# A decoder layer on one core: the second products of a tile group in a bank of their own, later table turning, and other rates for the weight sums

## The chip, the cores and the metric

The kernel runs on one core of a Trainium2 chip, as one launch. The metric is the device time of a run in microseconds. The kernel before took 1041.94 us (median of three runs: 1041.69, 1041.94, 1045.71). Everything said of single instructions comes from one further execution that the hardware profiler recorded.

## The reference

One layer of a decoder is computed for 512 positions of width 1024, in 32-bit floats. A combined projection gives queries, keys and values for three causal mixers and three gate vectors; the branches are projected, gated, summed and projected again; after a layer norm come a squared-ReLU MLP of width 4096, a gated embedding and a second layer norm. Cut to its frame:

```python
proj = x @ w_in
(da_q, da_k, da_v, sb_q, sb_k, sb_v, dl_q, dl_k, dl_v, gates) = jnp.split(proj, _split_points(), axis=-1)
...
o_da = diff_attention(da_q, da_k, da_v, lam, da_norm, rel_bias[:, :DA_HEADS], lam_init)
o_sb = stick_breaking_attention(sb_q, sb_k, sb_v)
o_dl = dilated_attention(dl_q, dl_k, dl_v, rel_bias[:, DA_HEADS:])
g = jax.nn.sigmoid(gates)
merged = g[0] * (o_da @ w_branch_da) + g[1] * (o_sb @ w_branch_sb) + g[2] * (o_dl @ w_branch_dil)
x = layer_norm(alpha * x + merged @ w_out, ln1_g, ln1_b)
c = jnp.square(relu(x @ w_up)) @ w_down
x = layer_norm(alpha * x + c + sigmoid(x @ w_ple_gate) * (p @ w_ple), ln2_g, ln2_b)
```

The differential attention (`da`) has four heads with two softmax maps each, the dilated one (`dl`) three groups of four heads. Both add a relative bias that depends on the distance alone; the kernel makes a table of it by loading shifted rows (tiles `sh`, from the DRAM vector `rv`) and reversing them on VectorE (tiles `shf`).

## The kernel before, in words

**Products.** Each 32-bit operand is split in a high and a low part, and each product is made of three matmuls: `mm3` (L87) issues them at L88, L89 and L90. Weights come in chunks of 128 x 1024 (512 KB): SyncE loads a chunk into `raw` (L214, six buffers), ScalarE (ACT) casts the high part `wh` (L262), VectorE (DVE) subtracts for the low part `wl` (L264). `wh` and `wl` have five buffers each, so the cast of a chunk waits for the last product with the chunk five before it.

**Seven instead of eight.** Most projections use a form with seven products on quarters of the operands instead of eight. It needs sums of weight quarters; these are made in DRAM by DMAs with addition that GpSimd (POOL) issues, in 200 steps: L1284 for a plain copy, L1282 for an addition. The tiles are `vsum`, `qsum`, `msum`, `bsum`, `gsum`, and for the MLP `usum` and `dsum`.

**The main stream.** The work is a list of items, each with its products (`mm`) and its evacuation (`ev`), which is recorded after the products of the next item have got their chunks. Per item n a credit grows by its size times its rate, and for each whole credit one sum step is issued; a manual dependency ties each step to a low part made shortly before. Attention heads are generators that are advanced a step at a time beside the items (`step()`); a generator in `pending` is advanced once a step too. The order on each engine is what comes of this recording and of a scheduler behind it, and is fixed before the run.

**Items.** The first are plain tiles, then three groups of eight items (`group_items`, at items 53, 61 and 69): a pair of dilated query and key tiles, differential heads 0 and 1, differential heads 2 and 3. Then come gates and branches: `gate_alone` (77 to 104), a first branch (105 to 112), `branch_seven` (113 to 126), `gate_chain` (127 to 140), `branch_seven` (141 to 158), the output projection, and the MLP from about item 180 to 317.

**One group.** For j = 0, 1 (two pairs of query and key tiles) the seven products, called by their numbers 1 to 7, are made with 128 x 256 results. Their order is: product 2 (`of_two`), 1 (`of_one`), 7 and 6 (`of_seven_six`), 5 (`of_five`), 3 and 4 (`of_three_four`). PSUM has two banks for results of this kind (`mm`) and six for all else (`at`, among them the attention logits). Product 2 goes into the left half (`HB`) of an `mm` bank, ACT copies it to `gs` (L419), and product 1 then goes into the same half of the same bank. DVE adds the two (`put`, L390, into `da_q` or `dl_q`); product 7, on the operand `u7h`, continues in this bank and so waits for the put. After the group, `doubled` makes the forms that the differential logits want: `da_qa`, `da_qb` from `da_q` (L102, L109, L110), then high and low parts of `da_k` (L401, L405 on ACT; L102 and L406 on DVE, tile `da_kl`). The logits are L147 and L148.

**Tables.** `da_tables` issues four loads of 256 KB on POOL (L1719) for the differential heads, at item `DA_TABS` = 58; `turn_da` records their four reversing copies on DVE (L1729), at item 62. The tables of the dilated heads were loaded the same way much earlier (items 9 to 22). L2052 adds a dilated table to logits, in softmax steps of a dilated head.

Of the kernel before, what the change touches and what calls it, by code (L numbers as in the profile page):

```python
# [13 lines left out]
AF = mybir.ActivationFunctionType  # L14
# [42 lines left out]
def trunk(tc, a, out):  # L57
    nc = tc.nc
    es = ExitStack()
    with es:  # L60
# [14 lines left out]
        def slot(name, dt=F32):  # L75
            return big.tile([P, 512], dt, name=nm(name), tag="s", bufs=NSLOT)
# [4 lines left out]
        def mm_bank():  # L81
            return psum.tile([P, 512], F32, name=nm("mm"), tag="mm", bufs=2)

        def at_bank():
            return psum.tile([P, 512], F32, name=nm("at"), tag="at", bufs=6)

        def mm3(ps, wh, wl, xh, xl, start, stop):  # L87
            nc.tensor.matmul(ps, wh, xh, start=start, stop=False, skip_group_check=True)  # L88
            nc.tensor.matmul(ps, wh, xl, start=False, stop=False, skip_group_check=True)  # L89
            nc.tensor.matmul(ps, wl, xh, start=False, stop=stop, skip_group_check=True)  # L90
# [193 lines left out]
        items = []  # L284
# [24 lines left out]
        scale = {"da_q": 0.125, "sb_q": 0.125, "dl_q": 128.0 ** -0.5}  # L309
# [39 lines left out]
        HB = slice(0, 256)  # L349
# [3 lines left out]
        def group_items(gi, pairs):  # L353
# [11 lines left out]
                    return ps.rearrange("p (n c) -> p c n", c=4)  # L365
                return ps

            def prod(j, p, c, start, stop):
                ch = cs[p][0]
                for k in range(4):  # L370
                    s = slice(512 * j + k * P, 512 * j + k * P + P)
                    mm3(both[j]["x"][:, c], ch["h"][:, s], ch["l"][:, s], *xf[p][k], start and k == 0, stop and k == 3)

            def add(ps, need, free, run, ev, bank):
                for p in ps:
                    at = {5: 0, 6: 1, 7: 2, 3: 3}.get(p)
                    cs[p] = [chunk(w[{1: 0, 2: 1, 4: 3}[p]] if at is None else qsum[gi][at], 1024)]
                item([c for p in free for c in cs[p]], lambda b: run(), lambda b: ev(),
                     need=[c for p in need for c in cs[p]], bank=bank)
                items[-1]["rate"] = 0.6  # L380
# [13 lines left out]
            def doubled(j):  # L394

                T[pairs[j][0]] = evac_stacked(out[j][0], "da_q", scale["da_q"])
                yield
                t = out[j][1]
                hi, lo = [[slot(n, F32R) for _ in range(2)] for n in ("da_k", "da_kl")]
                for i, c in enumerate((A, B)):  # L400
                    nc.scalar.activation(hi[i][c], t[c], AF.Copy, scale=-1.0)  # L401
                    sub_hi(lo[i][c], t[c], -1.0, hi[i][c])
                yield
                for i, (c, d) in enumerate(((A, B), (B, A))):
                    nc.scalar.copy(hi[i][d], hi[i][c].bitcast(F32))  # L405
                    nc.vector.tensor_copy(lo[i][d], lo[i][c].bitcast(F32))  # L406
                T[pairs[j][1]] = list(zip(hi, lo))
                yield

            def of_two():  # L410
                def run():
                    for j in range(2):
                        b = both[j]
                        if j:
                            b["x"] = mm_bank()
                        prod(j, 2, HB, True, True)
                        b["s"] = slot("gs")
                        sc = -scale[pairs[j][0][0]] if pairs[j][0][0] == "dl_q" else 1.0
                        nc.scalar.activation(b["s"][:, HB], b["x"][:, HB], AF.Copy, scale=sc)  # L419

                def ev():
                    for j in range(2):
                        for i in range(2):
                            out[j][i] = slot(pairs[j][i][0])

                def bank():
                    both[0]["x"] = mm_bank()
                    return both[0]["x"]
                add((2,), (2,), (2,), run, ev, bank)

            def of_one():
                def run():
                    for j in range(2):
                        prod(j, 1, HB, True, False)
                        if not j:
                            put(0, 0, 0, both[0]["x"][:, HB], both[0]["s"][:, HB])

                def ev():
                    put(1, 0, 0, both[1]["x"][:, HB], both[1]["s"][:, HB])
                add((1,), (1,), (1,), run, ev, lambda: both[0]["x"])  # L440

            def of_seven_six(j):
                def run():
# [327 lines left out]
        def seven(forms, operand, bank_of, done):  # L771

            cs = {}
            for p in (1, 2, 7, 6, 4, 5, 3):
                for r in range(2):
                    if not r:
                        cs[p] = [operand(cs, p, kp) for kp in range(2)]

                    def mm(ps, p=p, r=r):
                        q = slice(r * P, r * P + P)  # L780
                        for k in range(4):
                            c = cs[p][k // 2]
                            n = slice(k % 2 * 512, k % 2 * 512 + 512)
                            h, lo = forms[p][k]
                            go, end = k == 0 and p in bank_of["first"], k == 3 and p in bank_of["last"]
                            nc.tensor.matmul(ps, h[:, q], c["h"][:, n], start=go, stop=False, skip_group_check=True)
                            nc.tensor.matmul(ps, h[:, q], c["l"][:, n], start=False, stop=False, skip_group_check=True)  # L787
                            nc.tensor.matmul(ps, lo[:, q], c["h"][:, n], start=False, stop=end, skip_group_check=True)

                    def bank(p=p, r=r):  # L790
                        return bank_of["get"](p, r)

                    def ev(ps, p=p, r=r):
                        done(ps, p, r)
                    if p == 5:
                        bank_of.get("sums", set()).add(len(items))
                    item(cs[p] if r else [], mm, ev, need=cs[p], bank=bank, size=0.5)
                    items[-1]["rate"] = 1.0

        msum = [[[dram.tile([P, 1024], F32, name=f"msum{n}_{m}_{i}") for i in range(2)] for m in range(2)]  # L800
                for n in range(3)]
# [128 lines left out]
        def branch_seven(i, behind):  # L930

            s, b, cs = {}, {}, {}
            for p in (2, 1, 7, 6, 4, 5, 3):
                for r in range(2):
# [31 lines left out]
                        m = merged[to]  # L966
                        (nc.vector.tensor_add if p in (1, 3) else nc.vector.tensor_sub)(m, m, g)
                    item([cs[p]] if r else [], mm, ev, need=[cs[p]], bank=bank, size=0.25)
                    items[-1]["rate"] = 1.4
                    to = {2: (r, 0), 7: (r, 1), 6: (2 + r, 1), 4: (2 + r, 0)}.get(p)  # L970
                    if to:
                        def pre(to=to):
# [20 lines left out]

        last_plain = grouped_at[0]
        for j, it in enumerate(items):
            it.setdefault("rate", 1.8 if j < 12 else 2.8 if j < 27 else 1.8 if j < 28 else 0.0 if j < 31 else 2.6 if j < 49 else 2.1)

        gate_alone(0, 1)
        gate_alone(1, 2)
# [1186 lines left out]
                except StopIteration:  # L2186
                    pending.remove(g)

        DA_TABS = grouped_at[0] + 5
        sum_steps_ = sum_steps()  # L2190
        credit = 0.0
        plain_left[0] = last_plain
# [3 lines left out]
        for n, it in enumerate(items):  # L2196
# [51 lines left out]
                turn_tables()  # L2248
            if n == DA_TABS:
                da_tables()  # L2250
            if n == DA_TABS + 4:
                turn_da()
            if n == wout_at + 1:
                load_pT()
# [141 lines left out]
```

## Time and profile before

| what | us |
|---|---|
| runs, median (lowest, highest) | 1041.94 (1041.69, 1045.71) |
| the profiled execution, its time | 1044.54 |
| its span, first to last instruction | 1042.8 |
| PE busy in it | 1024.1 |
| DVE busy / ACT busy / POOL busy | 802.7 / 601.9 / 202.4 |
| moved by DMA | 266.55 MB |
| mean granted clock of PE | 0.995 |

How to read it: busy times are from the first part of the page; idle time of an engine costs something only where another engine, in the end PE, waits for it. The mean granted clock is the share of full speed that the chip let TensorE run at. The dilated group runs at about 332 to 354 us of the span, the first differential group to about 384, the second to about 415; the gate chain lies around 570.

### The profile page before, as it was taken

Reading aid. Unit: us, or ns where it says so; the run is one execution under the profiler, and the core shown is the slowest. Engines: PE = TensorE matmul, PEld = TensorE weight load, DVE = VectorE, ACT = ScalarE, POOL = GpSimd, SP = SyncE. Lnnn points to the kernel's source line nnn. Section 1 sums busy time; section 2 is a strip of 40 time slices with the busy share of each in tenths; the row PEclk is TensorE's granted clock in tenths of the full one; section 3 lists DMA queues with packets and bytes.
Section 4 is the critical chain, followed back from the end, with each engine's and each line's share of the span. In section 5 each row is a group of like instructions: output and inputs, shape, how many; then the busy total and the mean of one; then the engine's idle time right before and its main releaser. Section 6 shows DMA issues by size and latency. Waiting matters only on the chain.

```text
span 1042.8 us, 15610 instructions
## 1 busy us (share of the span) xinstructions
PE 1024.1 (98%) x5650; PEld 888.5 (85%) x5650; DVE 802.7 (77%) x1445; ACT 601.9 (58%) x1033; POOL 202.4 (19%) x307
## 2 busy tenths in 40 slices
PE   9999999999999999999999999999999999999996
PEld 7888888889988889888787888889999899899885
DVE  7888768668676678888877895898778777777975
ACT  7565444536335467756663853776666556556651
POOL 1222422241211211112222131212121111110001
PEclk9999999999999999999999999999999999999998
DMA  8989997997847968888999997599999999987522
GB/s 309 292 215 270 277 250 212 283 290 193 308 117 229 335 217 188 216 234 232 343 255 246 322 364 231 103 244 358 337 312 313 312 344 328 312 238 270 180 70 75
DMA packets 76205, 266.55 MB, mean 256 GB/s; under 512 B 9464, under 2 KB 10248, under 8 KB 76128
## 3 DMA queue, kind: packets, MB, share of 16 engines
q0 software_dynamic: 36624, 130.89, 49.8%
q1 hardware_dynamic: 38928, 133.75, 35.2%
q8 instruction: 44, 0.72, 0.3%
q10 hardware_dynamic: 576, 0.92, 0.2%
q14 instruction: 33, 0.27, 0.1%
HBM read 261.30 MB, written 109.08 MB: 355 GB/s over the span
## 4 chain that ended last, share of the span: by engine, by line
PE 86%; DMA 5%; DVE 3%; issue 2%; ACT 2%; POOL 1%; DVEq 0%; POOLq 0%; ACTq 0%
PE mm L88 9%; PE mm L89 9%; PE mm L90 9%; PE at L1465 4%; PE at L1466 4%; PE at L1467 4%; PE mm L650 2%; PE mm L648 2%; DMA sh<-rv 2%; PE mm L649 2%; DMA raw<-in_wgm_dram 2%; PE at L90 1%; PE at L89 1%; PE at L88 1%; PE at L787 1%
## 5 line engine op out<-in xcount | busy, mean ns | idle before, releaser
L262 ACT CAST wh<-raw 128x1024 fp32r<-128x1024 f32 x268 | 277.9, 1042 | 237.7 <-PE mm L89 121.0
L264 DVE TENSOR_TENSOR wl<-raw,wh 128x1024 fp32r<-128x1024 f32 x268 | 323.3, 1214 | 113.3 <-ACT wh L262 111.9
L88 PE MATMUL mm<-xhT,wh 128*128 128x512 f32 (+1 forms) x302 | 109.7, 363 | 1.4 <-ACT gs L419 1.1
L90 PE MATMUL mm<-xhT,wl 128*128 128x512 f32 (+1 forms) x302 | 108.4, 359 | 0.0
L89 PE MATMUL mm<-xlT,wh 128*128 128x512 f32 (+1 forms) x302 | 108.2, 358 | 0.0
L1465 PE MATMUL at<-wh,hh 128*128 128x512 f32 x188 | 73.7, 392 | 0.0
L1466 PE MATMUL at<-wl,hh 128*128 128x512 f32 x188 | 73.7, 392 | 0.0
L1467 PE MATMUL at<-wh,hl 128*128 128x512 f32 x188 | 73.1, 389 | 0.0
L88 PE MATMUL mm<-x1hT,wh 128*128 128x256 f32 x256 | 72.9, 285 | 0.0
L90 PE MATMUL mm<-x1hT,wl 128*128 128x256 f32 x256 | 72.4, 283 | 0.0
L89 PE MATMUL mm<-x1lT,wh 128*128 128x256 f32 x256 | 72.4, 283 | 0.0
L88 PEld LDWEIGHTS mm<-xhT,wh 128*128 128x128 f32 x302 | 57.7, 191 | 10.4 <-ACT gs L419 1.3
L90 PEld LDWEIGHTS mm<-xhT,wl 128*128 128x128 f32 x302 | 57.7, 191 | 8.3
L89 PEld LDWEIGHTS mm<-xlT,wh 128*128 128x128 f32 x302 | 57.8, 191 | 7.8
L1282 POOL DMA_DIRECT2D usum<-in_wu_dram x32 | 27.4, 857 | 131.5 <-DVE wl L264 71.6
L88 PEld LDWEIGHTS mm<-x1hT,wh 128*128 128x128 f32 x256 | 48.9, 191 | 1.9
L89 PEld LDWEIGHTS mm<-x1lT,wh 128*128 128x128 f32 x256 | 49.0, 191 | 1.5
L90 PEld LDWEIGHTS mm<-x1hT,wl 128*128 128x128 f32 x256 | 48.9, 191 | 0.0
L1282 POOL DMA_DIRECT2D dsum<-in_wd_dram x28 | 24.8, 886 | 100.7 <-DVE wl L264 40.6
L1467 PEld LDWEIGHTS at<-wh,hl 128*128 128x128 f32 x188 | 35.3, 188 | 7.7
L1465 PEld LDWEIGHTS at<-wh,hh 128*128 128x128 f32 x188 | 35.5, 189 | 6.2
L1466 PEld LDWEIGHTS at<-wl,hh 128*128 128x128 f32 x188 | 35.5, 189 | 5.7
(656 smaller groups left out, 2811.3 us busy)
## 6 DMA issues: line engine op xcount, KB each, us to landing
usum<-in_wu_dram POOLq DMA_DIRECT2D x48, 512.0 KB, 8.8
dsum<-in_wd_dram POOLq DMA_DIRECT2D x42, 512.0 KB, 9.3
raw<-usum SPq DMA_DIRECT2D x32, 512.0 KB, 7.7
raw<-dsum SPq DMA_DIRECT2D x28, 512.0 KB, 6.7
raw<-in_wt_dram SPq DMA_DIRECT2D x26, 512.0 KB, 6.6
raw<-in_wd_dram SPq DMA_DIRECT2D x25, 512.0 KB, 6.6
raw<-in_wu_dram SPq DMA_DIRECT2D x24, 512.0 KB, 7.2
raw<-in_wv_dram SPq DMA_DIRECT2D x18, 512.0 KB, 7.4
```

The source lines that it names most:

```text
L88: nc.tensor.matmul(ps, wh, xh, start=start, stop=False, skip_group_check=True)
L89: nc.tensor.matmul(ps, wh, xl, start=False, stop=False, skip_group_check=True)
L90: nc.tensor.matmul(ps, wl, xh, start=False, stop=stop, skip_group_check=True)
L262: i = nc.scalar.copy(h, raw)
L264: i = nc.vector.tensor_sub(lo, raw, h.bitcast(F32))
L648: nc.tensor.matmul(ps, x1, c["h"][:, s], start=k == 0, stop=False)
L649: nc.tensor.matmul(ps, x1, c["l"][:, s], start=False, stop=False)
L650: nc.tensor.matmul(ps, x2, c["h"][:, s], start=False, stop=k == 7)
L1282: i = nc.gpsimd.dma_start(o, i, accum_op=OP.add, max_dma_last_dim=4096)
L1465: nc.tensor.matmul(ps, h[:, q], c["h"][:, s], start=go, stop=False, skip_group_check=True)
L1466: nc.tensor.matmul(ps, h[:, q], c["l"][:, s], start=False, stop=False, skip_group_check=True)
L1467: nc.tensor.matmul(ps, lo[:, q], c["h"][:, s], start=False, stop=end, skip_group_check=True)
```

## The change

It has four parts.

1. *Own bank.* In `of_two` both second products go into one bank of the `at` kind, `both[0]["z"]`: that of j = 0 into the left half, that of j = 1 into the right half (`HC`). ACT copies each half to `gs`. `of_one` takes new `mm` banks.
2. *A step more.* `doubled` yields once more before it publishes `da_k`, so that the differential heads see it one step later.
3. *Rates.* Items before 12 issue sum steps at 2.7 instead of 1.8, items of `gate_alone` at 0.8 instead of 1.0, those of `branch_seven` at 1.0 instead of 1.4.
4. *Tables.* `da_tables` comes at item 55 instead of 58, `turn_da` at item 66 instead of 62.

```diff
-            def prod(j, p, c, start, stop):
+            def prod(j, p, c, start, stop, to=None):
                 ch = cs[p][0]
+                ps = (to or both[j]["x"])[:, c]
                 for k in range(4):
                     s = slice(512 * j + k * P, 512 * j + k * P + P)
-                    mm3(both[j]["x"][:, c], ch["h"][:, s], ch["l"][:, s], *xf[p][k], start and k == 0, stop and k == 3)
+                    mm3(ps, ch["h"][:, s], ch["l"][:, s], *xf[p][k], start and k == 0, stop and k == 3)
...
                     nc.vector.tensor_copy(lo[i][d], lo[i][c].bitcast(F32))
+                yield
                 T[pairs[j][1]] = list(zip(hi, lo))
                 yield
...
                 def run():
-                    for j in range(2):
-                        b = both[j]
-                        if j:
-                            b["x"] = mm_bank()
-                        prod(j, 2, HB, True, True)
-                        b["s"] = slot("gs")
+                    for j, c in enumerate((HB, HC)):
+                        prod(j, 2, c, True, True, both[0]["z"])
+                        both[j]["s"] = slot("gs")
                         sc = -scale[pairs[j][0][0]] if pairs[j][0][0] == "dl_q" else 1.0
-                        nc.scalar.activation(b["s"][:, HB], b["x"][:, HB], AF.Copy, scale=sc)
+                        nc.scalar.activation(both[j]["s"][:, HB], both[0]["z"][:, c], AF.Copy, scale=sc)
...
                 def bank():
-                    both[0]["x"] = mm_bank()
-                    return both[0]["x"]
+                    both[0]["z"] = at_bank()
+                    return both[0]["z"]
                 add((2,), (2,), (2,), run, ev, bank)
 
             def of_one():
                 def run():
                     for j in range(2):
+                        both[j]["x"] = mm_bank()
                         prod(j, 1, HB, True, False)
...
-                add((1,), (1,), (1,), run, ev, lambda: both[0]["x"])
+                add((1,), (1,), (1,), run, ev, lambda: None)
...
-                    items[-1]["rate"] = 1.0
+                    items[-1]["rate"] = 0.8
...
-                    items[-1]["rate"] = 1.4
+                    items[-1]["rate"] = 1.0
...
-            it.setdefault("rate", 1.8 if j < 12 else 2.8 if j < 27 else 1.8 if j < 28 else 0.0 if j < 31 else 2.6 if j < 49 else 2.1)
+            it.setdefault("rate", 2.7 if j < 12 else 2.8 if j < 27 else 1.8 if j < 28 else 0.0 if j < 31 else 2.6 if j < 49 else 2.1)
...
-        DA_TABS = grouped_at[0] + 5
+        DA_TABS = grouped_at[0] + 2
...
-            if n == DA_TABS + 4:
+            if n == DA_TABS + 11:
                 turn_da()
```

What this does to the order is seen at three places. Numbers behind a name tell one buffer from another; lines in rows of after are those of the changed kernel, one or two from those of before (L418 is L419 there, L391 is L390, L402 is L401, L407 is L406).

The first is PE in the second differential group; of each run of twelve equal rows (three matmuls by four) only the first stands here. Before, with `mm_796` and `mm_798` as the banks of the two pairs: product 2 is made with `wh_763`, product 1 with `wh_766`, product 7 with `wh_777`.

```order
L88 MATMUL mm_796_4000<-xhT_70,wh_763_3823 128x256
...
L88 MATMUL mm_798_4015<-xhT_70,wh_763_3823 128x256
...
L147 MATMUL at_816_4118<-da_k_790_3986,da_qa_782_3941 128x256
...
L88 MATMUL mm_796_4000<-xhT_70,wh_766_3829 128x256
...
L88 MATMUL mm_798_4015<-xhT_70,wh_766_3829 128x256
...
L147 MATMUL at_818_4123<-da_k_791_3987,da_qb_783_3942 128x256
...
L147 MATMUL at_826_4144<-da_k_791_3987,da_qb_783_3942 128x256
...
L88 MATMUL mm_796_4000<-u7h_651_3168,wh_777_3890 128x256
...
L88 MATMUL mm_798_4015<-u7h_651_3168,wh_777_3890 128x256
```

After, with `at_798` as the bank of product 2 and `mm_812`, `mm_813` as those of the pairs; product 2 is made with `wh_761`, product 1 with `wh_764`, product 7 with `wh_779`.

```order
L88 MATMUL at_798_4006<-xhT_70,wh_761_3821 128x256
...
L88 MATMUL mm_812_4058<-xhT_70,wh_764_3827 128x256
...
L88 MATMUL mm_813_4072<-xhT_70,wh_764_3827 128x256
...
L147 MATMUL at_823_4162<-da_k_792_3992,da_qa_784_3948 128x256
...
L147 MATMUL at_838_4203<-da_k_792_3992,da_qa_784_3948 128x384
L88 MATMUL at_798_4006<-xhT_70,wh_761_3821 128x256
...
L148 MATMUL at_838_4203<-da_kl_794_3994,da_qa_784_3948 128x384
L147 MATMUL at_840_4208<-da_k_793_3993,da_qb_785_3949 128x384
L148 MATMUL at_840_4208<-da_kl_795_3995,da_qb_785_3949 128x384
L88 MATMUL mm_812_4058<-u7h_651_3173,wh_779_3897 128x256
```

The right half of product 2 now stands behind both products 1 and behind the first logits, and only three logit matmuls lie between it and product 7.

The second is DVE and ACT at the same place, ahead of the put that product 7 waits for. ACT after, from the copy of the left half on (`gs_799`); `wh_814` is the chunk that takes the buffer of `wh_761`.

```order
L418 ACTIVATE gs_799_4019<-at_798_4006 128x256
L262 CAST wh_801_4035<-raw_755_3740 128x1024
L262 CAST wh_814_4085<-raw_763_3825 128x1024
L418 ACTIVATE gs_800_4033<-at_798_4006 128x256
L402 ACTIVATE da_k_808_4050<-da_k_745_3680 64x512
L406 CAST da_k_808_4050<-da_k_808_4050 64x512
L402 ACTIVATE da_k_809_4051<-da_k_745_3680 64x512
L406 CAST da_k_809_4051<-da_k_809_4051 64x512
```

Before, ACT copied both halves (`gs_797`, `gs_799`) with no cast between them:

```order
L262 CAST wh_800_4030<-raw_757_3742 128x1024
L109 ACTIVATE da_qa_794_3994<-da_q_744_3674 64x512
L110 ACTIVATE da_qb_795_3995<-da_q_744_3674 64x512
L419 ACTIVATE gs_797_4013<-mm_796_4000 128x256
L419 ACTIVATE gs_799_4028<-mm_798_4015 128x256
L405 CAST da_k_791_3987<-da_k_791_3987 64x512
L401 ACTIVATE da_k_807_4044<-da_k_745_3675 64x512
L405 CAST da_k_807_4044<-da_k_807_4044 64x512
L401 ACTIVATE da_k_808_4045<-da_k_745_3675 64x512
L405 CAST da_k_808_4045<-da_k_808_4045 64x512
```

The cast of two chunks has come between the two copies of product 2; the rest of ACT's rows kept their order. On DVE after, in the same stretch:

```order
L264 TENSOR_TENSOR wl_802_4036<-raw_755_3740,wh_801_4035 128x1024
L264 TENSOR_TENSOR wl_815_4086<-raw_763_3825,wh_814_4085 128x1024
L102 SCALAR_TENSOR_TENSOR da_kl_810_4052<-da_k_745_3680,da_k_808_4050 64x512
L407 CAST da_kl_810_4052<-da_kl_810_4052 64x512
L102 SCALAR_TENSOR_TENSOR da_kl_811_4053<-da_k_745_3680,da_k_809_4051 64x512
L391 TENSOR_TENSOR da_q_804_4041<-mm_812_4058,gs_799_4019 128x256
L391 TENSOR_TENSOR da_q_806_4043<-mm_813_4072,gs_800_4033 128x256
```

Before, the low part of the second chunk (`wl_812`) stood behind both puts; now (`wl_815`) it stands ahead of them.

The third is DVE in the first differential group, ahead of its first put. Before, with the reversing copies of the differential tables (L1729):

```order
L1729 COPY shf_746_3677<-sh_714_3522 128x512
L264 TENSOR_TENSOR wl_740_3667<-raw_707_3440,wh_739_3666 128x1024
L1729 COPY shf_747_3679<-sh_715_3524 128x512
L1729 COPY shf_748_3681<-sh_716_3526 128x512
L1729 COPY shf_749_3683<-sh_717_3528 128x512
L2052 ISA L12_730_3618,ma_752_3695<-at_750_3685,shf_338_1749 128x128
L2052 ISA ma_752_3695 128x1
...
L2052 ISA L12_731_3619,st_727_3615<-at_751_3686,shf_339_1751,ma_752_3695 128x128
L2052 ISA st_727_3615 128x1
L390 TENSOR_TENSOR da_q_742_3672<-mm_735_3636,gs_736_3649 128x256
```

After; the four reversing copies stand behind the put, near the end of the dilated head's softmax, and a low part (`wl_740`) stands among the L2052:

```order
L2052 ISA L12_731_3624,ma_748_3691<-at_746_3681,shf_338_1754 128x128
L2052 ISA ma_748_3691 128x1
L264 TENSOR_TENSOR wl_740_3672<-raw_708_3445,wh_739_3671 128x1024
L2052 ISA L12_731_3624,st_728_3621<-at_747_3682,shf_339_1756,ma_748_3691 128x128
L2052 ISA st_728_3621 128x1
L2052 ISA L12_731_3624,ma_748_3691<-at_746_3681,shf_338_1754 128x128
...
L2052 ISA L12_732_3625,ma_748_3691<-at_746_3681,shf_338_1754 128x128
L2052 ISA ma_748_3691 128x1
L391 TENSOR_TENSOR da_q_742_3677<-mm_751_3709,gs_737_3655 128x256
L2052 ISA L12_732_3625,st_728_3621<-at_747_3682,shf_339_1756,ma_748_3691 128x128
```

Of the eight table additions (each L2052 with a row that reads its maximum) one now stands ahead of that low part, six between it and the put, and one behind the put.

## The prediction

> **What bounds the kernel now.** I read the page first: the busy shares, the clock and the DMA row.
>
> ```profile
> span 1042.8 us, 15610 instructions
> PE 1024.1 (98%) x5650; PEld 888.5 (85%) x5650; DVE 802.7 (77%) x1445; ACT 601.9 (58%) x1033; POOL 202.4 (19%) x307
> PEclk9999999999999999999999999999999999999998
> DMA  8989997997847968888999997599999999987522
> ```
>
> TensorE is busy 98% of the span. The change takes no product away, so only its 18.7 us without work and the time at a lower clock can be won, and much of that is the start and the tail, which the change doesn't touch. So I looked for holes in the middle, with the busy time by stretches of 25 us around the three groups, the gates and the branches (columns: stretch, busy us of PE, PEld, DVE, ACT and POOL, granted clock, DMA share, GB/s).
>
> ```profile
> 350.00:375.00 25.00, 22.61 (x189) 22.26 (x188) 20.09 (x66) 13.84 (x33) 2.94 (x5) 1.00 0.92 327
> 375.00:400.00 25.00, 22.48 (x162) 21.61 (x162) 17.94 (x38) 16.15 (x31) 3.26 (x5) 0.93 0.70 232
> 400.00:425.00 25.00, 24.79 (x170) 22.32 (x169) 21.17 (x47) 20.75 (x45) 3.92 (x5) 1.00 0.75 170
> 500.00:525.00 25.00, 24.20 (x116) 19.71 (x115) 22.76 (x45) 18.60 (x36) 4.64 (x7) 1.00 1.01 309
> 550.00:575.00 25.00, 23.20 (x101) 18.49 (x101) 18.69 (x25) 9.43 (x12) 5.25 (x7) 1.00 1.00 245
> ```
>
> Two stretches in the groups lose 2.4 and 2.5 us, one of them at a clock of 0.93; one in the gate chain loses 1.8. The timeline of PE shows them one by one (start, duration; in brackets the idle time before, and what ended it).
>
> ```profile
> 364.59 0.39 PE L88 MATMUL mm<-u7h,wh 128*128 128x256 f32 x1 [2.39 <-DVE da_q L390]
> ...
> 386.07 0.39 PE L88 MATMUL mm<-xhT,wh 128*128 128x256 f32 x1 [0.24 <-ACT da_q L388]
> ...
> 389.07 0.38 PE L148 MATMUL at<-da_kl,da_qa 128*128 128x256 f32 x1 [1.18 <-DVE da_kl L406]
> 390.56 0.44 PE L88 MATMUL mm<-xhT,wh 128*128 128x256 f32 x1 [1.10 <-ACT gs L419]
> 390.80 0.42 PE L89 MATMUL mm<-xlT,wh 128*128 128x256 f32 x1
> 391.01 0.42 PE L90 MATMUL mm<-xhT,wl 128*128 128x256 f32 x1
> ...
> 394.31 0.28 PE L88 MATMUL mm<-xhT,wh 128*128 128x256 f32 x1
> 394.43 0.28 PE L89 MATMUL mm<-xlT,wh 128*128 128x256 f32 x1
> ```
>
> Idle here: 2.39 + 0.24 + 1.18 + 1.10 = 4.9 us. From 390.56 a product steps by 0.21 us and more, from 394.31 by 0.12: the 18 products between take 3.75 us instead of 2.16, 1.6 lost. **The groups hold 6.5 us** that the change can reach. The chain of waits shows where the largest hole comes from.
>
> ```profile
> 344.31 17.48 DMA sh<-rv
> 361.82 0.43 DVE shf L1729
> 364.19 0.35 DVE da_q L390
> ```
>
> The second tables took 17.48 us to land; VectorE stood at their reversing copy, and the put of da_q, which frees the bank for the seventh product, stood behind it.
>
> **The change part by part.** The sum starts at the profiled execution, 1044.54 us (span 1042.8 and 1.7 around it). That is 2.6 above the median of the runs shown, 1041.94, so what comes out is lowered by 2.6 at the end. These mean durations (ns, after the comma) price what stands in the queues of ACT and VectorE:
>
> ```profile
> L262 ACT CAST wh<-raw 128x1024 fp32r<-128x1024 f32 x19 | 19.7, 1045 | 11.4 <-PE mm L89 8.0 <-issue 2.9 <-ACT gs L419 0.5
> L401 ACT ACTIVATE da_k<-da_k 64x512 fp32r<-64x512 f32 x6 | 3.8, 625 | 0.1
> L405 ACT CAST da_k<-da_k 64x512 fp32r<-64x512 f32 x6 | 3.7, 617 | 0.2
> L419 ACT ACTIVATE gs<-mm 128x256 f32<-128x256 f32 x4 | 1.4, 378 | 0.0
> ...
> L264 DVE TENSOR_TENSOR wl<-raw,wh 128x1024 fp32r<-128x1024 f32 x20 | 24.2, 1221 | 8.1 <-ACT wh L262 7.8
> L102 DVE SCALAR_TENSOR_TENSOR da_kl<-da_k,da_k 64x512 fp32r<-64x512 f32 x6 | 4.1, 685 | 0.5 <-ACT da_k L401 0.4
> L390 DVE TENSOR_TENSOR da_q<-mm,gs 128x256 f32<-128x256 f32 x4 | 1.7, 422 | 0.7 <-PE mm L90 0.7
> L406 DVE CAST da_kl<-da_kl 64x512 fp32r<-64x512 f32 x6 | 2.5, 422 | 0.2
> L2052 DVE CUSTOM_DVE_ANT_0 L<-at,shf,ma 128x128 f32<-128x128 f32 x4 | 1.2, 348 | 0.0
> ```
>
> *Tables.* The 17.48 us of landing now begin three items sooner, and the four copies (0.42 each) stand eleven items behind the load. The 1.04 us that VectorE waited and the copies leave the put of da_q. On POOL the four loads stand behind four sum steps more than before, since the denser first steps have moved those ahead; with some 0.8 us of issue each (3.2) that doesn't use up the distance of eleven items. The copies come among the last softmax of the dilated branch, ahead of its second transposed tile, and cost PE there between 0 and 1.7 (four copies); I take 0.6.
>
> *Own bank, first differential group.* Next late is the put of da_q itself. Call t the end of the second half of the second products. Only there a weight buffer comes free; then follow the cast (1.05), its low part (1.22), about six products with a table (L2052, 0.21 to 0.35 each, 1.5) and the put (0.42): t + 4.2. PE has 22 products of 0.12 and some small ones, 3.1 us. It stands 1.1 where it stood 2.39. The second half waits for ACT's copy of the first, with two products and two small ones between: 0.4.
>
> *Own bank, second differential group.* The waits on gs and da_q (0.24 + 1.10) go, since the first products take other banks, and the one on da_kl shrinks from 1.18 to some 0.4, as 36 products instead of 24 stand before it. But those 24 first products now stand ahead of the second half, and no longer cover what follows it. From its end T: cast 1.05, gs copy 0.38, so T + 1.4; on this the logits that take the next bank wait, some 1.2 us. Then on ACT L401, L405, L401 (1.87), T + 3.3; on VectorE the low part is done at T + 2.3, L102 at T + 3.0, L406 at T + 3.4, the second L102 at T + 4.1, and the put of da_q at T + 4.5. The seventh product waits for it from T + 1.8: 2.7 us. **New idle time: 3.9 us.** The price lies between 0, if the cast isn't the last thing to come, and 6, if VectorE is behind as well; I take what the queue gives. What stands behind that put (the next low part, the logits' softmax) has slack.
>
> *The clock.* In before, 2.28 us idle within 3 us (1.18 and 1.10) halved the clock; 2.39 in one piece at 364.59 did not. 1.2 and 2.7 with 0.4 between should do it again: 1.6, as before. [...]
>
> *The extra step before da_k is published.* It delays the first logits by one step; their softmax has no PE wait over 0.4 us in the 25 us behind (24.79 busy): between 0 and 0.6, taken as 0, since the da_kl wait above already holds it.
>
> Stage of the groups after: 0.4 + 1.1 + 0.6 + 0.4 + 3.9 + 1.6 = 8.0, against 6.5: **+1.5**.
>
> *Thinner sum steps.* The gate chain's hole, PE first and then ACT:
>
> ```profile
> 569.02 0.49 PE L786 MATMUL at<-wh,u7h 128*128 128x512 f32 x1 [1.03 <-ACT wh L262]
> 570.28 0.50 PE L787 MATMUL at<-wl,u7h 128*128 128x512 f32 x1 [0.77 <-DVE wl L264]
> ```
>
> ```profile
> 563.16 1.05 ACT L262 CAST wh<-raw 128x1024 fp32r<-128x1024 f32 x1 [5.46 <-DMA raw<-in_wgm_dram]
> 567.92 1.99 ACT L262 CAST wh<-raw 128x1024 fp32r<-128x1024 f32 x2 [3.71 <-DMA raw<-in_wgm_dram]
> ```
>
> A weight chunk with an addition landed late at a DMA share of 1.00. The order on POOL around it is the same, but the steps are paced apart: two of eight go from this stretch. It can save all 1.80, or nothing; I take two thirds: **-1.2**. The two to three steps that end late fall on sums of the MLP, where PE waits for no sum in before.
>
> *Denser first steps.* Items 5 to 11 issue at 2.7 instead of 1.8. The DMA row reads 8 and 9 there and PE 9, and the rate of 2.8 already ran behind them; cost 0. The one chain that is pushed back is the first tables':
>
> ```profile
> L1719 POOL DMA_DIRECT2D sh<-rv x8: 726/796/869, 123.3 to 344.3; - x8
> ...
> DMA to landing us min/median/max: 6.0/11.0/17.5
> ```
>
> Issued from 123.3, they landed by 144 even with the longest landing, and their copies stand at 159.9. Four to six steps of some 0.8 us on POOL fit into that; without that cover each late us would cost one.
>
> The sum: 1044.54 + 1.5 - 1.2 = 1044.8; less 2.6: **1042.2**. In this program about 0.5% (5.2 us) is what a measurement can tell from no change, so this is "same".
>
> **The rivals.**
> [...]
> - *The bank does what it should*: ACT and VectorE are ahead, the freed buffer isn't the last thing, both puts come in time, and no dip follows. Idle time left: 0.4 + 0.6 + 0.4; 6.5 - 1.4 = 5.1 gained, and 1.2 of the gates: 1041.9 - 6.3 = **1035.6**. For it: ACT is busy only 16 of 25 us here. Against it: the buffer is freed by the very products that were moved back.
> - *The steps don't help the gate chain*, or the edit doesn't act there: its two chunks are issued in the same place of the queue and land as late: **1043.4**.
> - *Slower*: the chunk whose cast follows T isn't there in time. ACT's copy of gs and all behind it then wait for a load, as for the raw chunk at 567.92 (3.71), and a second half-clock stretch follows (1.6): 1042.2 + 5.3 = **1047.5**. It decides the sign from about 3.4 us of such a wait on. For it: the loads share the queues with sum steps that are now further ahead, at a DMA share of 0.92. Against it: 0.70 in the stretch in question.
>
> **How the numbers follow.** Forecast (waits change places, dip stays) 0.48; clock stays 0.14; bank does it all 0.18; gates don't gain 0.08; slower 0.12. Predicted: 1042.2. The third case lies mostly beyond 1036.7 and gives nearly all of "faster": 0.16. "Slower" (over 1047.2): 0.11; "same" 0.73. The range reaches from 1035.4, which holds most of the third case, to 1047.0, just short of the slower one; the new put's bounds (0 and 6 around 3.9) lie within it.
>
> **What would show it.** In after: no wait on sh behind L1729 in the groups; the 2.4 us on da_q gone from one place and a wait of 2 to 3 us on da_q in the next group, behind one of about 1 on gs; one stretch of half clock there, or none; the chunk waits near 563 to 568 under 3 us each. It would be wrong if PE has no wait on da_q in the second differential group, or if the time moves at a place outside the groups and the gates.

## The result, and the profile after

| what | us |
|---|---|
| before, median of 14 runs (lowest, highest) | 1042.24 (1040.29, 1047.99) |
| changed, median of 14 runs (lowest, highest) | 1046.18 (1044.48, 1049.91) |
| ratio of changed to before | 1.0032, interval 1.0017 to 1.0047 |
| profiled execution of the changed kernel, and its span | 1049.91, 1048.2 |

The changed kernel is slower by 0.32%: inside the bound of 0.5%, so "same" as the prediction has it, but clear of zero, and 4.0 us above the forecast of 1042.2. Its profiled execution is the slowest of its 14 runs, and that of its second profile (e12, below) took 1049.34, so what a part of the change is worth is taken from the times of the experiments and not from these two profiles.

The page of the changed kernel, the same rows as were shown of before:

```profile
span 1048.2 us, 15614 instructions
PE 1027.5 (98%) x5650; PEld 891.2 (85%) x5650; DVE 802.2 (77%) x1445; ACT 602.3 (57%) x1033; POOL 202.1 (19%) x307
PEclk9999999999999998999999999999999999999999
DMA  8999998996945978778999997489999999988522
```

No engine has more to do. What changed is where PE waits. The stretches of 25 us of the changed kernel (columns as before: PE, PEld, DVE, ACT, POOL busy, clock, DMA share, GB/s):

```profile
225.00:250.00 25.00, 23.26 (x110) 21.20 (x109) 18.55 (x56) 13.94 (x31) 2.56 (x5) 0.97 0.74 213
...
275.00:300.00 25.00, 22.88 (x121) 20.48 (x120) 12.83 (x44) 8.16 (x21) 9.03 (x13) 1.00 0.97 295
300.00:325.00 25.00, 23.56 (x146) 20.68 (x147) 21.93 (x78) 11.27 (x29) 1.12 (x2) 1.00 0.13 39
350.00:375.00 25.00, 24.31 (x200) 23.86 (x199) 15.31 (x44) 13.86 (x34) 4.13 (x6) 1.00 0.99 321
375.00:400.00 25.00, 23.51 (x184) 22.11 (x182) 19.73 (x43) 16.16 (x26) 2.78 (x4) 1.00 0.77 209
400.00:425.00 25.00, 22.25 (x147) 20.96 (x146) 20.27 (x56) 16.37 (x37) 4.25 (x5) 0.86 0.70 170
500.00:525.00 25.00, 25.00 (x131) 21.02 (x131) 22.57 (x46) 15.79 (x36) 4.67 (x7) 1.00 0.97 336
550.00:575.00 25.00, 25.00 (x112) 20.54 (x111) 24.43 (x34) 12.92 (x17) 5.39 (x7) 1.00 1.01 264
```

The holes at 500 and 550 are gone, those of the groups have moved by one stretch, and there are new ones between 225 and 325, where the prediction had named none. PE's own table of waits in the changed kernel (total, times, longest) says for what:

```profile
PE at L2073 <- DVE r L2065: 5.3, 2, 3.5
PE mm L88 <- DVE da_q L391: 3.3, 2, 2.6
...
PE at L147 <- ACT gs L418: 1.1, 1, 1.1
...
PE at L148 <- DVE da_kl L407: 0.2, 1, 0.2
```

**The groups** came out as worked out. Behind the right half of product 2 PE waits 1.13 on gs (forecast 1.2) and 2.63 on the put of da_q (forecast 2.7); the put in the group ahead holds it 0.66 (1.1). The timeline of PE in the changed kernel, and the clock around it by stretches:

```profile
399.67 0.44 PE L147 MATMUL at<-da_k,da_qb 128*128 128x384 f32 x1 [1.13 <-ACT gs L418]
399.95 0.34 PE L148 MATMUL at<-da_kl,da_qb 128*128 128x384 f32 x1
402.92 0.58 PE L88 MATMUL mm<-u7h,wh 128*128 128x256 f32 x1 [2.63 <-DVE da_q L391]
```

```profile
398.75:402.20 3.45, 0.62 (x2) 0.30 (x2) 2.98 (x5) 3.25 (x6) 1.86 (x3) 1.00 0.78 232
402.20:409.00 6.80, 6.08 (x28) 6.08 (x29) 4.68 (x24) 2.04 (x9) 0.41 (x1) 0.50 0.98 252
409.00:412.40 3.40, 3.40 (x27) 3.22 (x26) 2.17 (x5) 3.01 (x7) 0.00 (x0) 1.00 0.47 92
```

In 3.45 us PE works 0.62; half clock follows for 6.8 us, twice as long as was forecast for it. The right half did wait for the copy of the left one: its first matmul starts at 396.70, and ACT's copy of the left half runs from 396.24 for 0.39.

**The new hole** at 301 is a wait for r, a small operand of the dilated head's softmax (L2065 on DVE). On DVE's timeline of the changed kernel, r stands behind L749, which makes the first operand forms of the groups from `xr` and waits for its load:

```profile
299.88 1.36 DVE L749 TENSOR_TENSOR xr<-xr,xr 128x512 f32<-128x512 f32 x2 [3.92 <-DMA xr<-in_xT_dram]
301.16 0.18 DVE L2065 TENSOR_TENSOR r<-st,exf 128x32 f32<-128x32 f32 x1
```

In the profile of before the same two rows read

```profile
292.97 1.35 DVE L749 TENSOR_TENSOR xr<-xr,xr 128x512 f32<-128x512 f32 x2 [0.84 <-DMA xr<-in_xT_dram]
294.25 0.18 DVE L2065 TENSOR_TENSOR r<-st,exf 128x32 f32<-128x32 f32 x1
```

So DVE waited for this load before, too, and PE 0.44 for r: there was no slack. The loads of xr (eight, L529) are issued by POOL, behind sum steps. POOL's timeline before, then after:

```profile
278.69 0.52 POOL L1284 DMA_DIRECT2D bsum<-bsum  x1 [5.08 <-DVE wl L264]
281.68 0.57 POOL L716 DMA_DIRECT2D oT<-oT  x1 [2.47 <-ACT oT L2143]
282.25 5.68 POOL L529 DMA_DIRECT2D xr<-in_xT_dram  x8
```

```profile
282.53 0.81 POOL L1282 DMA_DIRECT2D bsum<-in_wbq_dram  x1 [4.79 <-DVE wl L264]
283.05 0.82 POOL L1284 DMA_DIRECT2D bsum<-bsum  x1
285.52 0.59 POOL L716 DMA_DIRECT2D oT<-oT  x1 [1.65 <-ACT oT L2143]
286.10 2.18 POOL L529 DMA_DIRECT2D xr<-in_xT_dram  x3
288.70 1.43 POOL L529 DMA_DIRECT2D xr<-in_xT_dram  x2 [0.42 <-issue]
291.50 0.71 POOL L529 DMA_DIRECT2D xr<-in_xT_dram  x1 [1.37 <-DMA bsum<-in_wbq_dram]
...
295.42 0.71 POOL L529 DMA_DIRECT2D xr<-in_xT_dram  x1 [1.16 <-PE at L2028]
```

Before, one plain copy of 512 KB stood ahead of the eight loads (with a transfer of `oT` between, as after), and they went out in one piece. After, an addition and a copy stand there, the sixth load waits until the addition has landed, and the last is issued 9.3 us behind the first. The median landing of the eight (the time from a transfer's issue until it has arrived) grows from 6.1 to 9.0 us.

### The profile page after: what moved, and what is told of

Same layout as the page of the kernel before. It is cut to its first block, busy times and chain, and to the rows that moved or that the text cites. A ratio compares the mean times of both kernels' runs of the same rounds, so it can differ in the third digit from the quotient of the medians.

```text
span 1048.2 us, 15614 instructions
## 1 busy us (share of the span) xinstructions
PE 1027.5 (98%) x5650; PEld 891.2 (85%) x5650; DVE 802.2 (77%) x1445; ACT 602.3 (57%) x1033; POOL 202.1 (19%) x307
## 3 DMA queue, kind: packets, MB, share of 16 engines
q0 software_dynamic: 36624, 130.89, 50.0%
q1 hardware_dynamic: 38928, 133.75, 34.7%
## 4 chain that ended last, share of the span: by engine, by line
PE 92%; DVE 2%; ACT 2%; issue 2%; DMA 2%; POOL 0%; DVEq 0%; ACTq 0%; POOLq 0%
PE mm L88 9%; PE mm L89 9%; PE mm L90 9%; PE at L1465 4%; PE at L1466 4%; PE at L1467 4%; PE at L786 2%; PE at L787 2%; PE at L788 2%; PE mm L650 2%; PE mm L648 2%; PE mm L649 2%; PE at L88 2%; PE at L89 2%; PE at L90 2%
## 5 line engine op out<-in xcount | busy, mean ns | idle before, releaser
L88 PE MATMUL mm<-xhT,wh 128*128 128x512 f32 (+1 forms) x278 | 101.4, 365 | 0.1
L90 PE MATMUL mm<-xhT,wl 128*128 128x512 f32 (+1 forms) x278 | 101.1, 364 | 0.0
L89 PE MATMUL mm<-xlT,wh 128*128 128x512 f32 (+1 forms) x278 | 100.9, 363 | 0.0
L88 PEld LDWEIGHTS mm<-xhT,wh 128*128 128x128 f32 x278 | 52.4, 189 | 8.5 <-ACT gs L450 0.3
L90 PEld LDWEIGHTS mm<-xhT,wl 128*128 128x128 f32 x278 | 52.5, 189 | 8.3
L89 PEld LDWEIGHTS mm<-xlT,wh 128*128 128x128 f32 x278 | 52.4, 189 | 7.8
```

## The experiments

Two theories. **A:** the denser first steps are what costs: they don't cost where they run, but shift which sum steps stand ahead of other transfers of POOL later, above all ahead of xr. **B:** the own bank alone makes the kernel slower, and the waits on r come and go with the run. The thinner rates and the tables had to be priced as well. All ratios are to runs of before that were taken beside them on the same chip.

**e1: the denser first steps taken back.**

```diff
-            it.setdefault("rate", 2.7 if j < 12 else 2.8 if j < 27 ...
+            it.setdefault("rate", 1.8 if j < 12 else 2.8 if j < 27 ...
```

> The changed kernel with the rate of the first items set back from 2.7 to 1.8, all else as changed. Theory A (the denser first steps delay transfers that stand behind sum steps on POOL): the waits of PE on r (1.74 at 247 and 3.52 at 301) fall below 1 us and 0.6 us, no half clock near 248, and the time falls by 4 to 6 us, to 1040 to 1042. Theory B (the own bank alone makes the kernel slower, and those waits only shift with the run): the time stays within 1.5 us of 1046.2. The sum steps end some eight steps late for the MLP; if that costs, PE waits for a wh there, which no run had so far.

Measured: 1042.43, ratio 0.9995 (0.9982 to 1.0008), so 3.8 us less than the changed kernel. PE's table of waits has no row on r any more; the waits of the groups stay within a hundredth (1.12 and 2.64). That is what theory A expects, with a time 0.4 above its range. POOL in this run shows one copy ahead of xr, as before, and a median landing of 6.1 us.

**e2: only the denser first steps, on the kernel before** (the same line, the other way round).

> The kernel before with the rate of the first items at 2.7 instead of 1.8, nothing else. Theory A: waits of PE on r at about 247 and 301 as in the changed kernel (1.7 and 3.5), and 4 to 6 us more, 1046 to 1049. Theory B: no such waits, 1042 within 1.5.

Measured: 1045.01, ratio 1.0011 (0.9996 to 1.0027). The wait on r at 297 is there:

```profile
PE at L2073 <- DVE r L2065: 2.9, 1, 2.9
```

That at 247 is not. The place is A's; the time is less than A expected, and its interval reaches zero. The gate chain's waits, which these rates don't touch, were gone here all the same: a first sign that they were not of the rates.

**e3: only thinner rates and moved tables, on the kernel before.**

```diff
-                    items[-1]["rate"] = 1.0
+                    items[-1]["rate"] = 0.8
...
-                    items[-1]["rate"] = 1.4
+                    items[-1]["rate"] = 1.0
...
-        DA_TABS = grouped_at[0] + 5
+        DA_TABS = grouped_at[0] + 2
...
-            if n == DA_TABS + 4:
+            if n == DA_TABS + 11:
```

> The kernel before with only the thinner rates (0.8 and 1.0) and the moved tables. If their gains are what the profiles show: the wait on da_q at 364 (2.4) and the gate chain's (1.8, and 0.8 at 510) go, 4 to 5 us less, 1037 to 1038.5. If sums that come eight steps late stall the MLP, or the gate chain's waits come from something else: 1040 or more.

Measured: 1039.76, ratio 0.9971 (0.9956 to 0.9985): **faster than both kernels**, if by less than expected. The wait on da_q fell from 2.39 to 0.20 us, and the two waits of the gate chain are gone; that of 0.80 near 510 (on `graw`), which was expected to go too, stays. From 600 to 900 us the sums are five or six steps behind those of before in the number issued, and PE waits for none of them.

**e4: the changed kernel with its second products in mm banks again** (`prod`, `of_two` and `of_one` as before the change, the rest as changed).

> The changed kernel with the second products in mm banks again, as before; rates, tables and the extra step as changed. If the own bank costs what the group stage shows (waits of 1.13 and 2.63 and 6.8 us of half clock, against 0.24, 1.18, 1.10 and 3.4 us): 2 to 4 us less, 1042 to 1044, and the two waits on r stay. If the bank is worth something: the time rises over 1047, with a wait on gs back in the groups.

Measured: 1043.98, ratio 1.0010 (0.9996 to 1.0024), 2.2 less than the changed kernel, which is at the lower end of what was expected. Against e3, from which it differs only by the denser start and the extra step, it costs 0.39% (4.2 us, the intervals lie apart): so the denser start is dear without the own bank, too. The wait on r stays (2.84), as A has it, and the waits of the second differential group are those of before:

```profile
PE at L148 <- DVE da_kl L406: 1.2, 1, 1.2
PE mm L88 <- ACT gs L420: 1.1, 1, 1.1
```

**e5: the first forms from xr recorded two steps later** (on the changed kernel).

```diff
-            for _ in range(5):
+            for _ in range(7):
                 yield
```

> The changed kernel with the first forms made of xr (L749 and behind) recorded two steps later on VectorE; their loads, the rates and all else as changed. Theory A, as the profile of the changed kernel has it: L749 waits 3.9 us for xr, whose loads POOL issues behind denser sum steps, and r (L2065), which PE waits for, stands behind L749. Then r no longer stands behind that wait: PE's wait on r near 301 is under 1 us, and the time falls by 2.5 to 4 us, to 1042.5 to 1043.5. Rival (the late loads hold back something else, or the DMA queues themselves): the wait moves to L749's next reader or stays, and the time stays within 1 us of 1046.2.

Measured: 1045.81, ratio 1.0034 (1.0022 to 1.0046): no gain. The profile shows why it says little: on DVE, L749 still stands ahead of r. The scheduler placed it as before, and only the loads and their wait were seen again:

```profile
295.94 0.69 DVE L749 TENSOR_TENSOR xr<-xr,xr 128x512 f32<-128x512 f32 x1 [2.77 <-DMA xr<-in_xT_dram]
297.05 0.69 DVE L749 TENSOR_TENSOR xr<-xr,xr 128x512 f32<-128x512 f32 x1 [0.41 <-DMA xr<-in_xT_dram]
297.66 0.18 DVE L2065 TENSOR_TENSOR r<-st,exf 128x32 f32<-128x32 f32 x1
```

That r is late *because* it stands behind L749 is thus read from the order and the trace, and not shown by an edit.

**e6 and e7: one own bank without the extra step, and two own banks.** Both have the rates and tables of e3. e6 is e1 without the added `yield`; e7 is e6 with

```diff
-                    for j, c in enumerate((HB, HC)):
-                        prod(j, 2, c, True, True, both[0]["z"])
+                    for j, c in enumerate((HB, HB)):
+                        if j:
+                            both[j]["z"] = at_bank()
+                        prod(j, 2, c, True, True, both[j]["z"])
...
-                        nc.scalar.activation(both[j]["s"][:, HB], both[0]["z"][:, c], AF.Copy, scale=sc)
+                        nc.scalar.activation(both[j]["s"][:, HB], both[j]["z"][:, c], AF.Copy, scale=sc)
```

> The kernel of e1_early_back without the extra step in doubled, so the kernel before with one own bank, thinner rates and moved tables. If the own bank alone costs what lies between e3_thin_and_tables (1039.8) and e1_early_back (1042.4): 1042 to 1043, with the waits on gs (1.1) and da_q (2.6) behind the right half. If the extra step is what costs: 1040 to 1041, and those waits shrink.

> The kernel of e6 with an own bank for each second product, two instead of one, both in the left half. If the cost of the own bank is that the right half must wait for ACT's copy of the left one, and so comes behind both first products: the two second products stand together again, no wait on gs, the wait on da_q of 2.6 falls under 0.7, no half clock in the groups in most runs, 1037 to 1038.5, so faster than both kernels. If the cost is any move of the second products out of the mm banks: 1042 or more. If the second bank starves the attention heads, which share those six: waits of PE at the logits, 1040 or more.

Measured: e6 1044.03, ratio 1.0013 (0.9999 to 1.0028); e7 1040.22, ratio 0.9974 (0.9961 to 0.9987). One own bank costs 0.42% over e3 (0.9971), two cost nothing that can be seen. So it isn't leaving the mm banks that costs, but sharing one. The extra step doesn't cost; e1, which has it, is rather below e6, and e6 is 1.0 above what was expected. e7, too, is slower than the 1037 to 1038.5 that were expected, and its waits are only half as expected:

```profile
PE mm L88 <- DVE da_q L391: 2.8, 1, 2.8
...
PE at L147 <- ACT da_k L406: 0.9, 1, 0.9
```

The wait on gs is gone, that on da_q is not, and 3.4 us of half clock still follow: the put now stands behind low parts and casts of the differential operands on a VectorE that has no gap over 0.05 us there, from 384.9 to 395.0. In the profile PE is busy 71.15 of the 75 us from 350 to 425 in e7 and 70.18 in e6, at clocks of 0.98 and 0.95. That is part of the 3.8 us between their medians. Where the rest is, one profile of each doesn't tell: these two executions (1041.58 and 1043.46) lie only 1.9 apart. So that sharing a bank costs is shown by the times; through which wait, only in part.

**e8: only the tables, on the kernel before.**

> The kernel before with only the moved tables. The wait on da_q at 364 (2.4) falls under 0.5, and so 1.5 to 2.5 us less than before, 1040 to 1041; the gate chain's waits (1.8) stay if the thinner rates are what removes them, and the half clock near 390 stays. If another wait takes the place: within 0.7 of before.

Measured: 1041.07, ratio 0.9989 (0.9978 to 1.0001). The wait on da_q at 364 fell to 0.20, as expected; the gain is 1.1 us, less than expected. The gate chain's waits are gone here as well, without any thinner rate.

**e9: two sum steps kept back, on the changed kernel.**

```diff
-                credit += it["size"] * it.get("rate", 1.0)
+                credit += 0.0 if 43 <= n < 47 else it["size"] * it.get("rate", 1.0) + 2.0 * (n == 49)
```

> The changed kernel with two sum steps kept back: items 43 to 46 issue none, and item 49 two more. So no sum step of 512 KB stands right ahead of the loads of xr on POOL, as two do in the changed kernel; from item 49 on everything is as changed, the five steps of lead too. Theory A (the denser start only shifts which steps meet the xr loads): the loads of xr start and land 3 us or more earlier, PE's wait on r near 297 to 301 falls under 1 us, and the time falls by 2 to 3.5 us, to 1042.7 to 1044.2. Rival (the lead as such costs, by DMA traffic or later): the wait or another of its size stays, 1045.5 or more.

Measured: 1048.71, ratio 1.0050 (1.0031 to 1.0068), the highest median of all. By the number that is the rival's side. POOL's timeline shows that the edit didn't do what was meant: two *additions* slid to the place of the two steps kept back,

```profile
278.94 1.64 POOL L1282 DMA_DIRECT2D gsum<-in_wg_dram  x2 [4.77 <-DVE wl L264]
281.92 0.60 POOL L716 DMA_DIRECT2D oT<-oT  x1 [1.34 <-ACT oT L2143]
282.50 2.89 POOL L529 DMA_DIRECT2D xr<-in_xT_dram  x4
285.69 0.73 POOL L529 DMA_DIRECT2D xr<-in_xT_dram  x1 [0.29 <-issue]
289.56 0.71 POOL L529 DMA_DIRECT2D xr<-in_xT_dram  x1 [3.14 <-DMA gsum<-in_wg_dram]
```

and PE's wait on r grew to 4.58. The lead in steps is the changed kernel's from item 49 on; what differs is what stands ahead of xr. So the run is no proof that the lead as such is free, but with the other profiles it orders three cases by what stands ahead of xr. Behind one copy the median landing is 5.5 to 6.6 us (before and the seven others that start at 1.8); behind an addition and a copy 7.9 to 9.5 (both profiles of the changed kernel, e2, e4, e5); behind two additions 10.4.

**e10: only the thinner rates. e11 and e12: both kernels once more**, for a second profile of each.

> The kernel before with only the thinner rates in gates and branches. If the thinning is worth the gate chain's waits: 1.5 us less than before or more, 1040.5, and no wait on wh or wl near 569. If those waits were of the one profiled execution: within 0.7 of before; then thinner rates and moved tables together (1039.8) are the tables' gain (1.1) and little else.

> The kernel before once more, for a second profile. If the profile that the prediction rests on shows what every run does: the waits at 364 (2.4), 389 (1.2), 390 (1.1), 569 (1.0) and 570 (0.8) again, within 0.3 each. If the gate chain's waits, or the size of that on da_q, hang on when transfers land: these differ by more than 0.5, the others not.

> The changed kernel once more, for a second profile. The waits that hang on the order alone (1.13 on gs, 2.63 on da_q) again within 0.1. The one on r near 301 (3.5) again over 2, since e2, e4 and e5 had it at 2.8 to 2.9. The one on r near 247 (1.7) not, since no other run with the denser start had it.

Measured: e10 1041.91, ratio 0.9995 (0.9979 to 1.0010): the thinner rates alone gain nothing that can be measured. In e11 (1041.33) the gate chain has one wait of 0.3, and da_q half of what the first profile had:

```profile
PE mm L88 <- DVE da_q L390: 1.3, 1, 1.3
...
PE at L148 <- DVE da_kl L406: 1.2, 1, 1.2
PE mm L88 <- ACT gs L419: 1.1, 1, 1.1
...
PE at L787 <- DVE wl L264: 0.3, 1, 0.3
```

What hangs on the order repeats to a tenth; what hangs on a landing does not. e12 (1049.34) has the waits of the groups again, that on r near 299 with 4.0, and none near 247 (that one was seen in a single profile, and what made it stays open):

```profile
PE at L2073 <- DVE r L2065: 4.0, 1, 4.0
PE mm L88 <- DVE da_q L391: 3.3, 2, 2.6
...
PE at L147 <- ACT gs L418: 1.1, 1, 1.1
```

**Theory A against B.** With the denser start (changed, e2, e4, e5, e9, e12) PE waits 2.8 to 4.6 us on r near 300 in all six profiles; with 1.8 (before, e1, e3, e6, e7, e8, e10, e11) 0 to 1.1 in all eight. The wait isn't the whole price: in four of the six (e4, e5, e9, e12) half clock stands at it, too, for 3.4 us in e4 and for 6.8 in the others. In e2 and in the first profile of the changed kernel there is none. The stretch at the wait in e12, then that behind it in e2:

```profile
296.80:303.60 6.80, 4.97 (x13) 4.01 (x14) 6.33 (x22) 2.08 (x9) 0.00 (x0) 0.50 0.11 43
297.10:304.00 6.90, 6.90 (x37) 5.83 (x38) 6.83 (x27) 2.56 (x10) 0.00 (x0) 1.00 0.00 0
```

So the denser start is shown to cost, and to come with the wait on r each time. That it costs through the sum steps ahead of xr is read from orders and landings: no edit moved those loads alone. B is right in that the own bank costs, too.

## Why the prediction was right or wrong

It was right that the change would make no difference of 0.5%, and the time lies in its range. It was wrong by 4.0 us, about the size of one term that it had at nothing. That the time still lies in the range is luck: its upper end, 1047.0, was drawn for late loads and waits in the groups, not for this. And one of the signs that the prediction named against itself came true: the time moved at a place outside the groups and the gates.

- **Denser first steps: forecast 0, measured +0.37% (3.8 us, e1 against the changed kernel); without the own bank +0.39% (e3 against e4, which has the extra step, too); on the kernel before, alone, +0.11% with an interval that reaches zero.** This is the step that failed. Why it is less on the kernel before stays open. The prediction looked for a cost at the items that issue the steps, and for transfers pushed back it named one chain, the tables', with its 16 us of cover. It did not follow the loads of xr, the other transfers that stand in POOL's queue behind sum steps, though the profile of before had the row: DVE waiting 0.84 us on xr, with r behind it. No cover there at all.
- **The stage of the groups: forecast +1.5, measured +1.4** (e8's tables gain 1.1, own bank and extra step add 0.24% or 2.5 us, e1 against e3). Its mechanism was right, and its two new waits were right to 0.1 us. That the sums agree to 0.1 us is partly luck: each ratio is known to about 0.13%, and the price of the one bank came out between 0.22% (e4 against the changed kernel) and 0.42% (e6 against e3). The put in the first differential group was forecast with 1.1 and waits 0.66; the half clock was forecast as one stretch of 3.4 us; it was 6.8 in the first profile of the changed kernel and in e6, and 3.4 in the second, in e1, e5 and e9.
- **The start of the sum.** The prediction took 2.39 as the wait on da_q, and at the end lowered the sum by 2.6, since that execution lay so far above the median. In three other profiles with the old table turning (e2, e10, e11) the wait is 1.28 or 1.29, which fits e8's gain of 1.1. Here and in the gate chain the first profile of before has 2.6 us more than the second, just what was taken off: it seems to have been counted twice, once as a gain and once in lowering the sum.
- **Clock.** The case "clock stays" (chance 0.14), in which no half clock follows the two new waits, fell: half clock (0.50 from 402.20 to 409.00 in the changed kernel) followed them in every profile with one own bank (changed, e1, e5, e6, e9, e12), with no single wait there over 2.7 us. The prediction's reading that waits of 1.18 and 1.10 are enough holds in only four of the seven profiles that have them (last section).
- **Thinner steps: forecast -1.2, measured -0.5 with an interval of -2.2 to +1.0 (e10).** The term was mis-sized, since it was taken from one execution: 1.8 us of waits in the first profile of before, 0.3 in the second, and none in e2 and e8, which have the old rates. The other side of the rates, sums that end late in the MLP, cost nothing, as forecast.
- **The extra step: forecast 0**; e1 against e6 gives -0.18% with overlapping intervals, so nothing against it. The step has an effect that the prediction didn't name: PE's wait of 0.80 on `graw` near 510 stands in all eight profiles without the step and in none of the six with it. That, and not the rates, is why the hole at 500 is gone; what it is worth in time is not shown.
- **"The bank does what it should"** fell: the buffer freed by the moved right half was what the queue waited for, as the argument against that rival had it. In e7, with a bank for each, the idea costs nothing that can be seen, but gains nothing either.
- The slower rival gave the right sign by the wrong way: no chunk's load was late in the groups. The price came 100 us earlier. That these loads share queues with the sum steps, as the prediction argues for this rival, no trace shows: SyncE issues the loads in question (L214) and POOL the steps, and the page of before has two large queues, of 130.89 and 133.75 MB.

The best version found is e3, tables and thinner rates alone; e7 is its equal within the intervals.

## What to carry to other kernels

When a change issues background transfers earlier, list every other transfer in the same queue, with the idle time of the engine that waits for it: one with no cover can cost more than all that was gained (here 0.37%, against the 0.29% that e3 gained), however far from the edit it stands. Two results in the halves of one buffer save a buffer, but in this program the second didn't start before the first was read, and sharing it cost 0.22 to 0.42%, more than the buffer was worth. A wait that hangs on a landing should be seen in two profiles before it is priced. One that hangs on the order of instructions repeats, and can be worked out from mean durations: here two of them to 0.1 us, a third (1.1 for 0.66) less well.

## What the runs showed that was not expected

**Half clock comes in stretches of 3.4 or 6.8 us.** Where the clock drops in the middle of the span, it does so for one of these two lengths (to 0.1), in all eleven profiles that have such a stretch; in the changed kernel the clock reads 0.50 from 402.20 to 409.00 and 1.00 from there to 412.40; it also reads 0.50 from 248.60 to 252.00. What sets the lengths is not shown.

**The same waits don't always halve the clock.** Before, e2, e3, e4, e8, e10 and e11 all have the waits of 0.24, 1.18 and 1.10 within 5 us of each other. In before, e4, e8 and e11 half clock followed, in e2, e3 and e10 it did not:

```profile
388.00:398.00 10.00, 8.74 (x65) 8.24 (x65) 9.45 (x26) 7.55 (x19) 1.66 (x2) 1.00 0.95 283
```

(e10, the stretch around and behind these waits, at a clock of 1.00.) At some 1.6 us each that can be part of the spread among runs of one kernel. Nor does the length of a single wait decide: those on r of 2.80 (e5) and 2.84 (e4) have half clock by them, those of 2.91 (e2) and 3.52 (changed, first profile) have none.

**The sixth load of xr waits for the sum step eight transfers ahead of it.** In all six profiles with the denser start the sixth load of xr is issued 0.5 to 0.6 us after the sum step that POOL issued eight transfers earlier has landed; the seventh follows the second sum step in the same way. In the changed kernel the addition is issued at 282.53 and lands 8.4 us later, at 290.9, and the sixth load goes out at 291.50. So here a slow addition held back the issue of the eighth transfer behind it. What makes POOL wait so, and whether it does so elsewhere, is not shown.
